# Conditioning loads in the order of need, and a second layer in three groups of units tied to the stream's quarters

## The chip, the cores and the metric

The kernel is one program on one core of a Trainium2 chip. The metric is the device time of one execution in microseconds (us). Before the change it is 3625.27 us, the median of three runs (3622.58 to 3629.86). The engines are named as in the profile: PE is the matrix engine, DVE the vector engine, ACT the scalar engine, POOL the engine that issues the indirect gathers, SP the queue that issues all other transfers.

## The reference

1024 tokens of width 1024 pass two layers. Each layer adds a mixer and then a mixture of experts to h; six vectors a layer (shift, scale and gate for each of the two) come from the conditioning vector c.

```python
c_act = silu(c)
for l in range(2):
    mod = c_act @ ada_w[l] + ada_b[l]                  # 1024 x 6144
    sh1, sc1, g1, sh2, sc2, g2 = split(mod, 6)
    hn = rms_norm(h) * (1 + sc1) + sh1
    if l == 0: mix = hgrn2_mixer(hn)                   # 8 heads, a state carried over the tokens
    else:      mix = stick_breaking_mixer(hn, k_sh, v_sh)   # a block of queries sees all keys before it
    h = h + g1 * mix
    hn = rms_norm(h) * (1 + sc2) + sh2
    h = h + g2 * peer_ffn(hn)
    if l == 0: k_sh, v_sh = split(modulated(rms_norm(h), c_act @ kv_ada_w) @ kv_w, 2)

def peer_ffn(xn):        # per token: 4 heads choose 16 of 16384 experts each
    s1, s2 = top16 of each half of the scores;  best, experts = top16 of the 256 sums
    hid = xn . u[expert]                               # 64 rows of u for each token
    return sum(softmax(best) * gelu(hid) * v[expert])  # 64 rows of v for each token
```

## The kernel before

The tokens are eight blocks of 128. The mixture of experts is a stream that starts in the second tenth of the program and runs to its end: for each layer and block 64 gathers, each of which brings one expert's u and v rows for 128 tokens (8 KB a token, 1 MB a gather) into a tile of the ring g, which has seven buffers. POOL issues the gather (L690), DVE multiplies it with the tokens' rows and sums (L692), ACT makes the weight and a 128 x 32 selection matrix (L694, L696), and PE adds the weighted v rows in PSUM (L699); this last reader sets the buffer free for the gather that is seven later. After 16 gathers DVE takes the sum out (L700). These 16 gathers are a quarter of a block (`peer_quarter`), and the text calls them a **slot**: 64 slots in all, numbered 0 to 63, of which 0 to 31 belong to layer 0.

Beside the stream the other work is done in groups of blocks. Layer 0's mixer (`hgrn_group`, then `mix_route`, which also picks the experts) runs in the groups G0 of two, three and three blocks, and the first of them stands ahead of the stream, because the first gather needs the experts of block 0. Layer 1's attention runs in two groups of four blocks (`attn_group`): queries, eight heads of keys, values and attention, the output (`mix_out`) and the choice of experts (`route_group`). It can start for a group when the stream of layer 0 has finished those blocks, and has to be done before the stream of layer 1 comes to them. Keys and values of the first group are written to memory and read back for the second; the weights are loaded once for each group, 512 KB at a time, into a ring wt of four tiles by SP.

The conditioning is `mod_cols`: each 512 KB piece of the matrix is loaded by SP and multiplied with c_act by one DVE instruction (L215). Twelve vectors of eight pieces (`ada`) and sixteen pieces for the shared keys (`kvada`) make 112 pieces, and all stand ahead of the first gather: 16 of them (`tail_mods`, the last two vectors of layer 1) after the first group's weights of the routing. Pieces after the first sixteen go through halves of one tile of the ring g (`half_tile`).

What decides the order: `at(t)` gives the instructions that follow a due time, and a scheduler orders each engine's instructions by it when the program is built; on the chip every engine then works in that order, and SP issues transfers in that order. T0 and PERIOD place the stream (207 us for a block), W0 the three groups of layer 0, W1 the two of layer 1. `tc.issue_after(x)` puts instructions behind x on their engine. Rings are `BUFS`: T and K are the tiles of a group's activations and of a head's keys, values and scratch; h holds the eight blocks' rows of h.

Of the kernel before, what the change touches and what calls it, by code (L numbers as in the profile page):

```python
# [21 lines left out]
G1 = [[0, 1, 2, 3], [4, 5, 6, 7]]  # L22
GH, GMAX = 3, 4
TAIL = 2
# [12 lines left out]
def tile_model(ctx, tc, x, cin, small, ada, w_in, w_out, kvada, kvw, sbq, sbo, wq, subk, tab0, tab1, out):  # L37
# [9 lines left out]
    BUFS = dict(wt=4, h=8, T=2, K=2, g=7, hn2=1, hq=2, gs=1, st=1)  # L47
# [141 lines left out]
    act_c = unit("hn2")  # L189
# [97 lines left out]
    def mix_out(oT, blocks, w_ap, l, t0, t1):  # L287
        n = len(blocks)
        at(t0)
        for half in range(2):  # L290
            at(t0 + (t1 - t0) * half / 2)
            gsb = mix_row(l, half)
            ws = [wload(w_ap[4 * half + c]) for c in range(4)]
            for i, b in enumerate(blocks):
                at(t0 + (t1 - t0) * (half * n + i) / (2 * n))
                ps = bank()
                for c in range(4):
                    for k in range(8):
                        T.matmul(ps[:, blk(c)], lhsT=oT[:, k, blk(i)], rhs=ws[c][:, k, :], start=(k == 0), stop=(k == 7))  # L299
                V.tensor_tensor(out=ps, in0=gsb, in1=ps, op=ALU.mult)  # L300
                hh = hts[b][:, 512 * half:512 * half + 512]
                V.tensor_tensor(out=hh, in0=hh, in1=ps, op=ALU.add)
# [7 lines left out]
    def hgrn_group(blocks, t0, t1):  # L310
# [27 lines left out]
    def mix_route(oT, blocks, gsb, spare, t0, t1):  # L338
# [7 lines left out]
        early_ws = []  # L346
        if blocks == G0[0]:
            work = [hts[7 - i] for i in range(n)]
            early_ws = hts[2:6]
# [17 lines left out]
        early = 1 if len(held) >= 8 else n  # L367
# [42 lines left out]
    def best_of(l, b, sc):  # L410
        eg = sm("eg", [128, 2, 64], bufs=GMAX)
# [126 lines left out]
    def route_group(l, blocks, t0, t1):  # L538
        at(t0)
# [7 lines left out]
        for j in range(8):  # L547
            at(t0 + 0.4 * (t1 - t0) * j / 8)
# [124 lines left out]
    def peer_quarter(l, b, q):  # L673
# [6 lines left out]
        for c in range(0, 16, NC):  # L680
# [32 lines left out]
    def attn_group(blocks, t0, t1):  # L713
        at(t0)
        d = t1 - t0
# [9 lines left out]
        for j in range(8):  # L725
            at(t0 + d * (0.02 + 0.09 * j / 8))
# [30 lines left out]
        mix_out(qT, blocks, sbo, 1, t0 + 0.7 * d, t0 + 0.8 * d)  # L757
        route_group(1, blocks, t0 + 0.8 * d, t1)
# [28 lines left out]
    def late_mods():  # L787
        mods_out(0)
        mod_cols(modk, kvada, 16, kvb, LATE)
        fold_gain(modk[:, 8:16], kvg)  # L790
        mods_mix(1, LATE)
        mod(1, 2, LATE)
        for m in range(3, 6 - TAIL):
            mod(1, m, LATE)

    def tail_mods():
        with after("tail"), after("wq"):
            for m in range(6 - TAIL, 6):
                mod(1, m, LATE)
# [97 lines left out]
```

## Time and profile before

| what | before |
|---|---|
| median of three runs | 3625.27 us (3622.58 to 3629.86) |
| the profiled execution: its time, its span | 3632.76 us, 3631.1 us |
| busy share PE, DVE, ACT, POOL | 71%, 72%, 31%, 42% |
| mean granted clock of PE | 0.805 |
| DMA: indirect gathers; all else that SP issues | 1073.81 MB, 74.6%; 195.69 MB, 14.3% |
| first gather; end of slot 0, 15, 17, 28, 31, 43, 46, 55 | 335.5; 408.5, 1275.5, 1380.5, 1988.2, 2109, 2783.1, 2932.0, 3299.8 us |

No engine is busy throughout; the busy shares are means over stages, and the slot ends (the start of L700, the first instruction after a slot's last weighted sum) cut the program into them. A DMA share of 1 means that the 16 DMA engines moved data all the time; the granted clock of 1 would be the full 2.4 GHz all the time, and 0.5 the 1.2 GHz.

### The profile page before, as it was taken

The page shows a single profiled execution, that of the slowest core. Times are in us where ns is not written, and L with a number is a line of the kernel's source. Part 1 is how long each engine was busy: PE and PEld are TensorE (multiplying, and loading weights), DVE is VectorE, ACT ScalarE, POOL GpSimd, SP SyncE. Part 2 cuts the span into 40 slices and gives each one's busy share as a digit, 9 for nine tenths or more (in the row PEclk, how much of TensorE's full clock was granted, in tenths as well). Part 3 has the DMA queues.
Part 4 walks back from the last instruction along what each step waited for, and adds up shares of the span by engine and source line. Part 5 has one row for each costly group of instructions (what it writes and reads, how often), then busy time and mean ns, then how long its engine had stood idle before and what let it go on. Part 6 is the DMA issues. An engine that isn't in the chain of part 4 may idle for free.

```text
span 3631.1 us, 52700 instructions
## 1 busy us (share of the span) xinstructions
PE 2585.4 (71%) x18916; PEld 1654.3 (46%) x18916; DVE 2600.6 (72%) x6229; ACT 1127.5 (31%) x2959; POOL 1523.5 (42%) x1691
## 2 busy tenths in 40 slices
PE   5787999878998888988933488788797333343433
PEld 4686666665767745557411135455573111111111
DVE  7949777599776896665799546766757985565555
ACT  2114332233322443333333233333333232222221
POOL 3322656335664333224334433343343444444443
PEclk8898999899999999999955589899998555555555
DMA  9845989897999899888889988887898899999998
GB/s 394 347 143 221 354 344 359 336 352 303 358 361 365 337 344 372 326 337 328 342 349 353 414 352 351 346 328 309 320 381 345 333 373 409 419 415 418 416 416 349
DMA packets 203878, 1272.86 MB, mean 351 GB/s; under 512 B 22626, under 2 KB 22754, under 8 KB 72547
## 3 DMA queue, kind: packets, MB, share of 16 engines
q0 software_dynamic: 147456, 1073.81, 74.6%
q1 hardware_dynamic: 56162, 195.69, 14.3%
q8 instruction: 152, 2.49, 0.3%
q14 instruction: 108, 0.88, 0.1%
HBM read 1261.02 MB, written 8.39 MB: 350 GB/s over the span
## 4 chain that ended last, share of the span: by engine, by line
PE 42%; DVE 28%; issue 13%; POOL 6%; DMA 6%; ACT 5%; POOLq 0%; SPq 0%; DVEq 0%; ACTq 0%; another core or an unknown queue 0%
DVE g L692 8%; PE pj L445 7%; PE va L699 6%; POOL g L690 5%; DMA g<-in_tab_dram,ev 5%; PE pj L730 3%; PE ps L299 3%; PE pj L747 3%; PE pj L552 3%; PE ps L362 2%; ACT hq L668 2%; PE pj L751 2%; PE pj L449 2%; PE po L783 2%; DVE g L215 2%
## 5 line engine op out<-in xcount | busy, mean ns | idle before, releaser
L690 POOL DMA_INDIRECT g<-in_tab_dram,ev x1024 | 1200.7, 1173 | 1720.1 <-PE va L699 1129.0
L692 DVE SCALAR_TENSOR_TENSOR g<-g,hq 128x1024 f32<-128x1024 f32 x1024 | 1260.7, 1239 | 298.7 <-DMA g<-in_tab_dram,ev 287.5
L699 PE MATMUL va<-g,sel 128*32 128x256 f32 x8192 | 751.0, 499 | 772.4 <-ACT sel L696 764.3
L699 PEld LDWEIGHTS va<-g,sel 128*32 128x32 f32 x8192 | 256.7, 132 | 1191.5 <-ACT sel L696 989.3
L694 ACT ACTIVATE w<-hid 128x2 f32<-128x2 f32 x512 | 104.2, 204 | 1293.2 <-DVE g L692 1274.5
L445 PE MATMUL pj<-T,wt 128*128 128x384 f32 (+1 forms) x1152 | 358.7, 462 | 0.0
L668 ACT COPY hq<-hn 32x1024 f32<-32x1024 f32 x256 | 266.8, 1042 | 44.6 <-DVE g L692 40.4
L696 ACT ACTIVATE sel<-dg,w 128x32 f32<-128x32 f32 x1024 | 273.0, 314 | 15.6
L445 PEld LDWEIGHTS pj<-T,wt 128*128 128x128 f32 x1152 | 216.6, 195 | 101.3 <-issue 7.2
L685 DVE TENSOR_TENSOR dg<-delta,gt 128x128 f32<-128x128 f32 x256 | 78.1, 305 | 179.7 <-ACT sel L696 179.2
L494 POOL TENSOR_TENSOR K<-K,F 128x384 f32<-128x384 f32 (+1 forms) x144 | 151.4, 1071 | 52.9 <-DVE T L466 35.4
L215 DVE SCALAR_TENSOR_TENSOR g<-g,hn 128x1024 f32<-128x1024 f32 x104 | 129.2, 1266 | 6.1 <-DMA g<-in_ada_dram 6.1
L449 PE MATMUL pj<-wt,T 128*128 128x128 f32 x1024 | 127.5, 280 | 0.7 <-ACT K L451 0.6
L751 PE MATMUL pj<-wt,T 128*128 128x128 f32 x1024 | 126.3, 277 | 0.0
L751 PEld LDWEIGHTS pj<-wt,T 128*128 128x128 f32 x1024 | 120.0, 192 | 12.7 <-issue 10.6
L449 PEld LDWEIGHTS pj<-wt,T 128*128 128x128 f32 x1024 | 120.5, 194 | 8.8 <-issue 3.7
L299 PE MATMUL ps<-wt,T 128*128 128x128 f32 x1024 | 123.8, 280 | 0.0
L299 PEld LDWEIGHTS ps<-wt,T 128*128 128x128 f32 x1024 | 118.3, 194 | 11.3 <-issue 9.5
L747 PE MATMUL pj<-T,wt 128*128 128x512 f32 x256 | 120.3, 619 | 0.0
L730 PE MATMUL pj<-T,wt 128*128 128x512 f32 x256 | 117.3, 610 | 2.1 <-DVE T L277 2.1
L552 PE MATMUL pj<-T,wt 128*128 128x512 f32 x256 | 116.2, 604 | 0.5 <-DVE T L277 0.5
L783 PE MATMUL po<-K 128*128 128x128 f32 x576 | 104.5, 329 | 15.4 <-ACT K L781 14.9
(239 smaller groups left out, 3896.2 us busy)
## 6 DMA issues: line engine op xcount, KB each, us to landing
wt<-in_w_in_dram SPq DMA_DIRECT2D x96, 512.0 KB
g<-in_ada_dram SPq DMA_DIRECT2D x88, 512.0 KB
g<-in_tab_dram,ev POOLq DMA_INDIRECT x1024
wt<-in_kvw_dram SPq DMA_DIRECT2D x32, 512.0 KB
wt<-in_w_out_dram SPq DMA_DIRECT2D x18, 512.0 KB
wt<-in_wq_dram SPq DMA_DIRECT2D x17, 512.0 KB
g<-in_kvada_dram SPq DMA_DIRECT2D x16, 512.0 KB
wt<-in_sbq_dram SPq DMA_DIRECT2D x16, 512.0 KB
```

Of the source, the lines that this page charges most:

```text
L299: T.matmul(ps[:, blk(c)], lhsT=oT[:, k, blk(i)], rhs=ws[c][:, k, :], start=(k == 0), stop=(k == 7))
L445: T.matmul(pw, lhsT=w[:, k, :], rhs=hT[:, k, 0:W], start=(k == 0), stop=(k == 7))
L449: T.matmul(ps[:, blk(i)], lhsT=hT[:, k, blk(i)], rhs=w[:, k, :], start=(k == 0), stop=(k == 7))
L552: T.matmul(ps[:, 0:128 * n], lhsT=w[:, k, :], rhs=hT[:, k, 0:128 * n], start=(k == 0), stop=(k == 7))
L668: S.copy(t[32 * j:32 * j + 32, :], hn2[32 * q:32 * q + 32, :])
L690: G.indirect_dma_start(out=t, out_offset=None, in_=tab, in_offset=bass.IndirectOffsetOnAxis(ap=ev[:, q, c + k:c + k + 1], axis=0))
L692: V.scalar_tensor_tensor(u, u, 1.0, hq, op0=ALU.mult, op1=ALU.mult, accum_out=hid[:, k:k + 1])
L696: S.activation(sel[:, k, :], dg[:, c % 4 + k, :], AF.Copy, scale=wt[:, k:k + 1])
L699: T.matmul(va[32 * m:32 * m + 32, 0:256], lhsT=sel[:, k, :], rhs=ts[k][:, 1024 + 256 * m:1280 + 256 * m], start=(c + k == 0), stop=(c + k ...
L730: T.matmul(ps[:, 0:W], lhsT=w[:, k, :], rhs=hT[:, k, 0:W], start=(k == 0), stop=(k == 7))
L747: T.matmul(ps[:, 0:W], lhsT=w[:, k, :], rhs=hT[:, k, 0:W], start=(k == 0), stop=(k == 7))
L751: T.matmul(ps[:, blk(i)], lhsT=hT[:, k, blk(i)], rhs=w[:, k, :], start=(k == 0), stop=(k == 7))
```

## The change

**Conditioning.** The 32 pieces of layer 1's vectors 2 to 5 (its mixer's gate and all that its experts need) leave the part ahead of the first gather and are loaded and multiplied inside the hgrn group of blocks 2 to 4, four pieces a head, through the tiles of h that belong to blocks 5 and 6; c_act is kept in block 7's tile so long. The due times of what stays ahead of the first gather are spread (60, 150, 240 in place of 30 and 60), and those of layer 0's groups and of the stream are 40 us earlier. `tail_mods` is gone.

**Layer 1.** The groups are [0,1,2], [3,4,5], [6,7]. `attn_group` becomes a generator that yields after each of twelve units: queries and norms, eight heads, two halves of the output, routing. Behind every slot of the stream from S1 = 17, 29 and 41 on, one unit of that group is put in, and PE's instructions of the unit come behind the last weighted sum of the slot (`after("va")`).

**Tiles.** A group tile T is 3072 columns in place of 4096 for a partition, the ring K has three tiles in place of two, the ring g six in place of seven.

```diff
-G1 = [[0, 1, 2, 3], [4, 5, 6, 7]]
-GH, GMAX = 3, 4
-TAIL = 2
+G1 = [[0, 1, 2], [3, 4, 5], [6, 7]]
+GH, GMAX = 3, 3
-T0, PERIOD = 305.0, 207.0
-W0 = [(5, 230), (250, T0 + 2 * PERIOD - 25), (T0 + 1.8 * PERIOD, T0 + 5 * PERIOD - 60)]
-W1 = [(T0 + 4.7 * PERIOD, T0 + 8.2 * PERIOD), (T0 + 7.9 * PERIOD, T0 + 11.8 * PERIOD)]
+T0, PERIOD = 265.0, 207.0
+W0 = [(5, 240), (210, T0 + 2 * PERIOD - 25), (T0 + 1.8 * PERIOD, T0 + 5 * PERIOD - 60)]
+S1 = [17, 29, 41]
-    BUFS = dict(wt=4, h=8, T=2, K=2, g=7, hn2=1, hq=2, gs=1, st=1)
+    BUFS = dict(wt=4, h=8, T=2, K=3, g=6, hn2=1, hq=2, gs=1, st=1)
...
         for hd in range(8):
             at(t0 + 0.67 * d * hd / 8)
             hgrn_head(n, hd, hT, oT, r8, [])
+            if blocks == G0[1]:
+                m = 2 + hd // 2
+                if hd % 2 == 0:
+                    acc1 = sm("macc", [128, 16])
+                for g in range(4 * (hd % 2), 4 * (hd % 2) + 4):
+                    w = hts[5 + g % 2]
+                    load(w, ada[1, 8 * m + g])
+                    V.scalar_tensor_tensor(w, w, 1.0, act_c, op0=ALU.mult, op1=ALU.mult, accum_out=acc1[:, g:g + 1])
+                if hd % 2:
+                    V.tensor_add(modc[1][:, 8 * m:8 * m + 8], acc1[:, 0:8], adab[:, 48 + 8 * m:56 + 8 * m])
+                    if m == 4:
+                        fold_gain(modc[1][:, 32:40], nfg[:, 8:16])
...
-    def attn_group(blocks, t0, t1):
-        at(t0)
-        d = t1 - t0
+    def attn_group(blocks):
...
+        yield
         for hd in range(8):
-            at(t0 + d * (0.12 + 0.58 * hd / 8))
...
             for i, b in enumerate(blocks):
                 attn_head(b, qT[:, hd, blk(i)], kh, vh, th, st)
-        mix_out(qT, blocks, sbo, 1, t0 + 0.7 * d, t0 + 0.8 * d)
-        route_group(1, blocks, t0 + 0.8 * d, t1)
+            yield
+        for half in range(2):
+            mix_half(qT, blocks, sbo, 1, half)
+            yield
+        route_group(1, blocks)
+        yield
...
-    at(30)
+    at(60)
     mods_ffn(0)
-    at(60)
-    late_mods()
+    at(150)
+    mods_out(0)
+    at(240)
+    mod_cols(modk, kvada, 16, kvb, LATE)
+    fold_gain(modk[:, 8:16], kvg)
+    mods_mix(1, LATE)
...
             peer_quarter(l, b, q)
-        for grp, w in zip(G1, W1):
-            if l == 0 and grp[-1] == b:
-                attn_group(grp, *w)
+            slot = 4 * n + q
+            for first, group in work:
+                if slot >= first:
+                    at(T0 + PERIOD * (slot + 1) / 4)
+                    with after("va"):
+                        next(group, None)
```

Three places show how this moves instructions. The first is SP's queue ahead of the first gather, behind the weights of the first group's routing. Before, it holds the last pieces of conditioning (g is a half tile of the ring g), between the w_in weights (wt) of the second group's heads:

```order
L93 DMA g_398<-in_ada_dram 128x1024 x2
L93 DMA wt_1084<-in_w_in_dram 128x1024
L93 DMA g_403<-in_ada_dram 128x1024 x2
L93 DMA g_408<-in_ada_dram 128x1024 x2
L93 DMA g_415<-in_ada_dram 128x1024 x2
L93 DMA g_420<-in_ada_dram 128x1024 x2
L93 DMA g_425<-in_ada_dram 128x1024 x2
L93 DMA g_430<-in_ada_dram 128x1024 x2
L93 DMA wt_1162<-in_w_in_dram 128x1024
L93 DMA wt_1180<-in_w_in_dram 128x1024
```

With the change, the same place holds the second group's rows (h_142 to h_144 are the tiles of blocks 2 to 4) and the first of the 32 moved pieces, which alternate between the tiles of blocks 5 and 6 (h_145 and h_146):

```order
L93 DMA wt_2327<-in_w_in_dram 128x1024
L93 DMA wt_2345<-in_w_in_dram 128x1024
L93 DMA h_142<-in_x_dram 128x1024
L93 DMA h_143<-in_x_dram 128x1024
L93 DMA h_144<-in_x_dram 128x1024
L93 DMA wt_2359<-in_w_in_dram 128x1024
L93 DMA h_146<-in_ada_dram 128x1024 x4
L93 DMA wt_2387<-in_w_in_dram 128x1024
L93 DMA h_146<-in_ada_dram 128x1024
L93 DMA h_145<-in_ada_dram 128x1024
L93 DMA wt_2490<-in_w_in_dram 128x1024
```

Sixteen pieces are gone from here, and every later piece stands among the weights of its head. The second place is DVE just ahead of the `gt` copy, which is the last thing that the first gather waits for (ev and gt are the experts' numbers and gates of block 0, s and ix the best scores and their places). Before:

```order
L569 MAX_INDEX ix_2151<-s_2150,h_146 128x8
L574 TENSOR_TENSOR cand_2162<-s_2150 128x256
L569 MAX_INDEX ix_2184<-s_2183,h_146 128x8
L613 CAST ev_7255<-pq_7238 128x64
L615 COPY gt_7257<-pq_7238 128x64
```

With the change (h_146 and h_147 in L333 are a moved piece and c_act; lines have moved by six there, so that L621 is the copy that was L615):

```order
L595 SCALAR_TENSOR_TENSOR eg_1829<-e_313_1959 128x16
L571 MAX s_2107<-h_145 128x8 x2
L571 MAX s_2140<-h_145 128x8 x2
L572 MAX_INDEX ix_2108<-s_2107,h_145 128x8 x2
L572 MAX_INDEX ix_2141<-s_2140,h_145 128x8 x2
L333 SCALAR_TENSOR_TENSOR h_146,macc_2480<-h_146,h_147 128x1024
L573 MATCH_REPLACE h_145<-s_2107,h_145 128x128 x2
L573 MATCH_REPLACE h_145<-s_2140,h_145 128x128 x2
L619 CAST ev_7241<-pq_7224 128x64
L621 COPY gt_7243<-pq_7224 128x64
```

The multiplies of moved pieces now stand between the pieces of the top-16 search; three of them stand ahead of this copy. The third place is PE in the middle of a slot that carries a head of layer 1 (va is the stream's weighted sum, T a group's activations, wt weights, K a head's tile, ps and po scores and output of one block's attention). Before, in slot 36:

```order
L783 MATMUL po_16529<-K_16411 128x128 x4
L747 MATMUL pj_16586<-T_15996,wt_16583 128x512 x8
L783 MATMUL po_16529<-K_16411 128x128 x2
L699 MATMUL va_19384<-g_19452,sel_19451 32x256 x4
L699 MATMUL va_19384<-g_19455,sel_19451 32x256 x4
L699 MATMUL va_19384<-g_19474,sel_19473 32x256 x4
L699 MATMUL va_19384<-g_19477,sel_19473 32x256 x4
L783 MATMUL po_16529<-K_16411 128x128
L751 MATMUL pj_16599<-wt_16596,T_15996 128x128 x14
L699 MATMUL va_19384<-g_19494,sel_19493 32x256 x4
L699 MATMUL va_19384<-g_19497,sel_19493 32x256 x4
L751 MATMUL pj_16599<-wt_16596,T_15996 128x128 x12
```

With the change, at the border from slot 23 to slot 24 (L751, L755 and L705 are the lines that were L747, L751 and L699):

```order
L705 MATMUL va_12053<-g_12205,sel_12204 32x256 x4
L705 MATMUL va_12053<-g_12208,sel_12204 32x256 x4
L751 MATMUL pj_12230<-T_10862,wt_12228 128x384 x8
L705 MATMUL va_12374<-g_12380,sel_12379 32x256 x4
L705 MATMUL va_12374<-g_12383,sel_12379 32x256 x4
L755 MATMUL pj_12243<-wt_12241,T_10862 128x128
L705 MATMUL va_12374<-g_12400,sel_12399 32x256 x4
L705 MATMUL va_12374<-g_12403,sel_12399 32x256 x4
L755 MATMUL pj_12243<-wt_12241,T_10862 128x128 x17
L705 MATMUL va_12374<-g_12422,sel_12421 32x256 x4
L705 MATMUL va_12374<-g_12425,sel_12421 32x256 x4
L755 MATMUL pj_12243<-wt_12241,T_10862 128x128 x5
```

Keys for three blocks are eight matmuls of 384 columns in place of 512 for four, and the head's work comes in one run from the border of a slot on, with the stream's weighted sums between its pieces. Before, pieces of the heads stood all over the slot, in the order that the scheduler's due times gave.

## Rows read from the trace of the kernel before

**Rows 1.** The page: busy time, share and instructions of each engine; the queue that SP fills (MB, share).
```profile
PE 2585.4 (71%) x18916; PEld 1654.3 (46%) x18916; DVE 2600.6 (72%) x6229; ACT 1127.5 (31%) x2959; POOL 1523.5 (42%) x1691
...
q1 hardware_dynamic: 56162, 195.69, 14.3%
```

**Rows 2.** Stretches: window, us, busy PE PEld DVE ACT POOL, PEclk, DMA share, GB/s.
```profile
0.00:335.50 335.50, 248.84 (x1539) 221.22 (x1540) 253.01 (x594) 76.65 (x169) 95.13 (x224) 0.89 0.70 268
409.50:1276.50 867.00, 783.60 (x6021) 572.78 (x6020) 679.43 (x1671) 283.95 (x769) 443.89 (x574) 0.95 0.89 345
1276.50:1381.50 105.00, 88.00 (x447) 40.86 (x447) 92.52 (x304) 45.46 (x103) 39.99 (x40) 0.92 0.94 357
1381.50:1989.50 608.00, 450.41 (x3321) 280.84 (x3323) 444.89 (x1234) 206.24 (x539) 217.10 (x196) 0.83 0.89 343
1989.50:2110.50 121.00, 48.80 (x440) 16.96 (x436) 70.91 (x130) 31.96 (x88) 56.83 (x51) 0.53 1.01 412
2110.50:2784.50 674.00, 583.00 (x4027) 372.16 (x4019) 439.81 (x820) 237.39 (x625) 254.30 (x215) 0.93 0.86 336
2784.50:2933.50 149.00, 49.95 (x446) 18.65 (x446) 145.57 (x531) 42.10 (x105) 65.86 (x55) 0.54 0.90 345
2933.50:3301.50 368.00, 145.62 (x1248) 48.77 (x1248) 224.25 (x439) 98.60 (x268) 169.42 (x154) 0.52 1.01 412
3301.50:3632.00 330.50, 125.63 (x1064) 40.30 (x1056) 185.82 (x333) 76.52 (x227) 141.92 (x133) 0.52 0.96 397
```

**Rows 3.** The same stretches, L700 alone (x is the slots that end there), PEclk, DMA share, GB/s.
```profile
409.50:1276.50 867.00, 6.31 (x15) 0.95 0.89 345
1381.50:1989.50 608.00, 4.67 (x11) 0.83 0.89 343
2110.50:2784.50 674.00, 5.13 (x12) 0.93 0.86 336
2784.50:2933.50 149.00, 1.27 (x3) 0.54 0.90 345
2933.50:3301.50 368.00, 3.87 (x9) 0.52 1.01 412
```

**Rows 4.** Timeline around the first gather: start and duration in us, then the instruction.
```profile
335.53 1.23 POOL L690 DMA_INDIRECT g<-in_tab_dram,ev  x1 [29.73 <-DVE gt L615]
...
341.35 1.23 DVE L692 SCALAR_TENSOR_TENSOR g<-g,hq 128x1024 f32<-128x1024 f32 x1 [0.35 <-DMA g<-in_tab_dram,ev]
```

**Rows 5.** The conditioning's multiply, by form: busy us, mean ns, idle before it.
```profile
L215 DVE SCALAR_TENSOR_TENSOR g<-g,hn 128x1024 f32<-128x1024 f32 x104 | 129.2, 1266 | 6.1 <-DMA g<-in_ada_dram 6.1
...
L215 DVE DVE_READ_ACCUMULATOR g<-g,hn 128x1 f32 x104 | 8.4, 81 | 0.0
```

**Rows 6.** Matmuls by form, each trace record standing for one of two per instruction.
```profile
L699 PE MATMUL va<-g,sel 128*32 128x256 f32 x8192 | 751.0, 499 | 772.4 <-ACT sel L696 764.3 <-issue 3.4 <-ACT w L694 3.3
L445 PE MATMUL pj<-T,wt 128*128 128x384 f32 x768 | 265.1, 493 | 0.0
...
L747 PE MATMUL pj<-T,wt 128*128 128x512 f32 x256 | 120.3, 619 | 0.0
L445 PE MATMUL pj<-T,wt 128*128 128x256 f32 x384 | 93.6, 400 | 0.0
```

**Rows 7.** Timeline of one tile of ring g in the stretch that starts at 3301.5 us.
```profile
3303.07 1.05 POOL L690 DMA_INDIRECT g<-in_tab_dram,ev  x1 [0.30 <-issue]
...
3315.70 1.23 DVE L692 SCALAR_TENSOR_TENSOR g<-g,hq 128x1024 f32<-128x1024 f32 x1 [1.21 <-DMA g<-in_tab_dram,ev]
...
3321.38 1.28 POOL L690 DMA_INDIRECT g<-in_tab_dram,ev  x1 [3.62 <-PE va L699]
```

**Rows 8.** Issues of transfers: how many, KB each.
```profile
wt<-in_kvw_dram SPq DMA_DIRECT2D x32, 512.0 KB
...
kD<-K SPq DMA_DIRECT2D x8, 256.0 KB
```

**Rows 9.** Waits over the program: us in all, times, longest.
```profile
POOL g L690 <- PE va L699: 1129.0, 329, 13.9
```

More of the change, by code (lines that the diff above doesn't have):

```diff
@@ L188, in tile_model @@
     V.scalar_tensor_tensor(crow, trow, 1.0, crow, op0=ALU.add, op1=ALU.mult)
-    act_c = unit("hn2")
+    act_c = hts[7]
     for half in range(2):
@@ L285, in mix_row, with mix_half @@
         return g
-    def mix_out(oT, blocks, w_ap, l, t0, t1):
-        n = len(blocks)
-        at(t0)
[L290 to L302, printed above, removed]
+    def mix_half(oT, blocks, w_ap, l, half):
+        gsb = mix_row(l, half)
+        ws = [wload(w_ap[4 * half + c]) for c in range(4)]
+        for i, b in enumerate(blocks):
+            ps = bank()
+            for c in range(4):
+                for k in range(8):
+                    T.matmul(ps[:, blk(c)], lhsT=oT[:, k, blk(i)], rhs=ws[c][:, k, :], start=(k == 0), stop=(k == 7))
+            V.tensor_tensor(out=ps, in0=gsb, in1=ps, op=ALU.mult)
+            hh = hts[b][:, 512 * half:512 * half + 512]
+            V.tensor_tensor(out=hh, in0=hh, in1=ps, op=ALU.add)
     state = unit("st", (128, 8, 128))
@@ L346, in mix_route @@
         early_ws = []
+        if blocks != G0[2]:
+            held += parts(ktile())
         if blocks == G0[0]:
-            work = [hts[7 - i] for i in range(n)]
-            early_ws = hts[2:6]
+            work = [hts[6 - i] for i in range(n)]
+            early_ws = hts[2:5]
         else:
@@ L365, in part_mix @@
             V.tensor_tensor(out=hh, in0=hh, in1=ps, op=ALU.add)
-        early = 1 if len(held) >= 8 else n
+        early = 1 if len(held) > 8 else n
         for half in range(2):
@@ L410, in best_of @@
     def best_of(l, b, sc):
-        eg = sm("eg", [128, 2, 64], bufs=GMAX)
+        eg = sm("eg", [128, 2, 64], bufs=4)
         for j in range(8):
@@ L536, in tile_model, with route_group @@
     norm00, norm7, best0 = [], [], []
-    def route_group(l, blocks, t0, t1):
-        at(t0)
+    def route_group(l, blocks):
         n = len(blocks)
@@ L547, in route_group @@
         for j in range(8):
-            at(t0 + 0.4 * (t1 - t0) * j / 8)
             w = wload(wq[l, j])
@@ L698, in peer_quarter @@
                 for m in range(4):
-                    T.matmul(va[32 * m:32 * m + 32, 0:256], lhsT=sel[:, k, :], rhs=ts[k][:, 1024 + 256 * m:1280 + 256 * m], start=(c + k == 0), stop=(c + k == 15))
+                    last["va"] = T.matmul(va[32 * m:32 * m + 32, 0:256], lhsT=sel[:, k, :], rhs=ts[k][:, 1024 + 256 * m:1280 + 256 * m], start=(c + k == 0), stop=(c + k == 15)).ins
         V.tensor_tensor(out=va[:, 0:256], in0=gates[l], in1=va[:, 0:256], op=ALU.mult)
@@ L725, in attn_group @@
         for j in range(8):
-            at(t0 + d * (0.02 + 0.09 * j / 8))
             w = wload(sbq[j])
@@ L784, in attn_head @@
         S.activation(qT, po[:, 0:128], AF.Copy, scale=0.5)
[L787 to L799, printed above, removed]
-            fold_gain(modc[1][:, 32:40], nfg[:, 8:16])
     at(0)
-    mods_mix(0, ["half"] * 8 + hts[2:] + parts(ktile())[:2])
-    at(30)
+    mods_mix(0, ["half"] * 8 + hts[2:7] + parts(ktile())[:3])
+    at(60)
     mods_ffn(0)
-    at(60)
-    late_mods()
+    at(150)
[4 more added lines that the diff above has]
+    mods_mix(1, LATE)
     for grp, w in zip(G0, W0):
         hgrn_group(grp, *w)
-        if grp is G0[0]:
-            at(240)
-            tail_mods()
     at(200)
@@ L818, in tile_model @@
     order = [(l, b) for l in range(2) for b in range(8)]
+    work = [(first, attn_group(grp)) for first, grp in zip(S1, G1)]
     with tc.issue_after(norm00[0]):
```

2 lines of the change are left out of this document (removed).

## The prediction

> **What bounds the kernel now.** I read the stretches first, because the shares of the page [rows 1] mix stages: PE and DVE look alike there, 71% and 72%, and bound different places. Dividing each stretch [rows 2] by the slots that end in it [rows 3] gives a slot's price by stage. Ahead of the first gather, 335.5 us, nothing streams; DVE is busy 253 of them and the DMA share is 0.70. From 409.5 to 1276.5 us layer 0's groups lie beside the stream: 15 slots of 57.8 us, PE busy 90%, so PE is the bound. While a group of layer 1 runs, slots take 56.2 us (674/12) with PE at 86%, and 55.3 us (608/11) in the first group. Three slots that carry the search for the best experts take 49.7 us with DVE at 98%. With nothing beside the stream a slot takes 40.9 us (368/9), DMA share 1.01: the gathers themselves are the bound, and PE is 40% busy at a granted clock of 0.52. So the program is a sum over slots, and the floor of a slot is 40.9 us. The chain of waits says the same of the stream: the largest wait of POOL is for the weighted sum that frees a buffer [rows 9].
>
> The important thing in these rows is that before, a slot is either full (56 us) or free (41). After the change 26 slots have a head of layer 1 each and are half full. Whether a half-full slot costs as little as its free DMA time allows decides the result.
>
> **Ahead of the first gather.** 16 of 112 pieces leave the part that the group's heads wait for, 16 more leave a place behind its routing. Sixteen pieces are 16 x (1.266 + 0.081) = 21.5 us of DVE [rows 5]; their loads are 16 x 1.39 = 22 us of the DMA engines (14.3% of 3631.1 us for 195.69 MB is 2.65 us a MB [rows 1], so 1.39 us for 512 KB). The stretch is 75% DVE, so not all of DVE's time is on the path: bounds 0 and 22 us. Against it, three moved multiplies stand ahead of the `gt` copy for which the first gather waits [rows 4], 3 x 1.35 = 4 us and some waiting for their loads, 6 in all. I take -22 + 6 = -16: the first gather at 319.5 us. Slot 0 was 73 us (335.5 to 408.5); by the order, 17 us more of layer 0's PE work stand ahead of its end, half of it in PE's idle time: +8, so it ends at 400.5.
>
> **Slots 1 to 17.** Layer 0's PE work is the same, and by the order it now ends with slot 14 in place of 15. A slot takes 11.7 us of stream work on PE (751.0/64 [rows 6]), so the same PE work without that slot is at most 867 - 11.7 = 855 us for slots 1 to 14; by slots it is 14 x 57.8 = 809. I take 840, nearer the PE bound. The 32 moved multiplies, 32 x 1.35 = 43 us, are put at nothing: DVE idles 188 of the 867 us [rows 2]. Without that cover they cost up to 43 us. Slot 15 has the search (55 us), slots 16 and 17 are free (82). Slot 17 ends at 400.5 + 840 + 137 = 1377.5, before 1380.5; the earlier start is nearly given back here, because the stage is bound by PE and slots 15 to 17 were partly filled before (105 us for two [rows 2]).
>
> **Slots 18 to 63.** Before these take 3632 - 1381.5 = 2250.5 us. By the order and the durations of such rows, after has 26 slots with one head (20 to 28, 33 to 40, 44 to 52) and 15 to 26 us of layer work on PE, 19.5 in the mean; 12 with the queries, the output and the routing, mostly 25 to 49 us on PE or 55 to 74 on DVE; and 8 free ones. The same count puts 40 us into each of before's twelve mixed slots. Narrower groups cost PE nothing: 384 columns take 265.1/384 = 0.69 us an instruction, 512 take 120.3/128 = 0.94, 256 take 93.6/192 = 0.49 [rows 6], all 1.8 to 1.9 ns a column.
>
> The bytes: the weights of layer 1 are loaded for three groups in place of two, 16 loads more of kvw beside its 32 [rows 8] and 25 of the others, 21.5 MB; keys and values written and read back grow by 7.3 MB. 28.8 MB x 2.65 = 76 us of DMA engines. In slots with PE as the bound they are hidden (DMA share 0.86 to 0.89); in half-full slots they are not.
>
> A light slot: lower bound, its DMA work alone, 40.9 + 2 loads x 1.39 + 0.39 to 0.79 MB of keys and values x 2.65 = 45. Upper bound, that the layer's PE work costs the stream what it costs now: (56.2 - 40.9) x 19.5/40 = 7.5 more than free, 48.4. I take **46.5**, the middle, since PE with (19.5 + 11.7)/46.5 = 67% is not the bound, but its pieces still come in between. A heavy slot 56.5, as now. A free slot 41.3: 26 x 46.5 + 12 x 56.5 + 330.5 = 2217.5, **-33 us**, of which 76 us of bytes are already paid.
>
> The ring with six buffers: a free slot asks for a gather every 2.56 us, so a buffer of seven comes round in 17.9 us (18.3 in the rows, 3303.07 to 3321.38 [rows 7]), one of six in 15.3. From the multiply to the new issue it takes 5.7 us, so 9.6 remain from issue to multiply; alone a gather takes 5.8 (335.53 to 341.35 [rows 4]). 3.8 us are left in place of 6.4, so free slots stay at 41. The last eight are 330.5 as before.
>
> **The sum.** Span 1377.5 + 2217.5 = 3595; 1.7 us around it make 3597. The profiled execution lies 7.5 us above the median of its runs (3632.76 and 3625.27), so on the median's scale it is **3590 us**. A measurement tells differences from about 0.2%, 7 us.
>
> **A rule against the change.** Rows: the granted clock is 0.52 where PE is 40% busy, 0.83 at 74%, 0.93 at 86% [rows 2]; on that line 67% busy would get 0.75 or so, a mix of 1.2 and 2.4 GHz, and 19.5 us of work become 24, still under the slot's 46.5. The Trainium skill, page "TensorE: Matmul & The Clock Gate", Part 1 on the clock gate, says that the slow clock is the default, that sustained activity lifts it and that idle gaps bring it back. By it, spread heads would run at the slow clock throughout. The trace agrees as far as it goes; no stretch of it shows half-full slots. As a mechanism of this kernel it is part of the third rival.
>
> **The rivals.**
> - *Full filling (0.20).* The head's PE work disappears in the stream's idle PE: light slots 45, heavy 54 (their loads, too, are earlier). -39 - 30 us: 3521. For it: free slots leave PE 60% idle. Against: before, no slot with layer work was under 45.
> - *Work is conserved (0.12).* Each piece costs the stream what it costs now, and the bytes come on top: light 48.4, 3590 + 26 x 1.9 = 3639. For it: the two groups of before differ little per us of work (55.3 and 56.2).
> - *The ring and the border piece (0.13), the slower side.* At each slot's border a piece of 8 x 0.69 = 5.5 us stands ahead of the stream's sums, over the 3.8 us that the ring of six leaves; seven buffers left 6.4. At the clock of the free slots, 0.52 in place of 0.93, the piece is near 10 us and 19.5 us of work are 35, with 16 of stream (145.6/9 [rows 2]) 51. Light slots of 49.8, between: 3590 + 26 x 3.3 = 3676. It decides from a light slot of 47.9 up. Against: PE's order keeps stream sums between the later pieces.
> - *Conditioning waits (0.07).* DVE works in order; a moved multiply whose load is late (two tiles, SP's queue between weights) holds the stream's multiplies behind it: up to +43 us in slots 1 to 14, 3633.
>
> **How the numbers follow.** The forecast as worked out, 3560 to 3618, has 0.36; the same mechanism with light slots of 47.6 to 48.1, within 7 us of before, 0.12. Faster is 0.36 + 0.20 = 0.56; same 0.12; slower 0.12 + 0.13 + 0.07 = 0.32. The likeliest case's own range is 3560 to 3618; the range for 8 in 10 reaches over the rivals on both sides, 3520 to 3685.
>
> **What would show it.** Right: the first gather near 320, slot 17's end near 1378, slots 20 to 28 of 46 to 47 us with a DMA share of 0.95 or more, free slots of 41 with six tiles. Wrong: light slots of 49 or more with a granted clock near 0.55 and more of POOL's wait for the weighted sum; a DVE that waits for loads at L333; or a first gather still at 335, if PE's heads and not the pieces set that stretch (PE is busy 249 of 335.5 us).

## The result and the profile after

The changed kernel takes 3720.43 us (median of four runs, 3716.19 to 3735.8), the kernel before 3627.57 us (3622.58 to 3630.07): a ratio of 1.0271 (95% interval 1.0254 to 1.0288), slower by 93 us between the medians and by 98 us by the ratio. The forecast was 3590 us with a range of 3520 to 3685. The profiled execution took 3716.99 us with a span of 3715.0 us.

The page after, engines and the queue that SP fills:

```profile
PE 2633.0 (71%) x19308; PEld 1770.2 (48%) x19308; DVE 2614.4 (70%) x6229; ACT 1137.9 (31%) x2993; POOL 1530.6 (41%) x1691
...
q1 hardware_dynamic: 66674, 224.53, 16.1%
```

Beside [rows 1] nothing stands out: the same shares, and 28.84 MB more. Stretches of the changed kernel (window, us, busy PE PEld DVE ACT POOL, PEclk, DMA share, GB/s): ahead of the first gather, slots 1 to 14, slots 15 to 17, the three runs of light slots, and the end.

```profile
0.00:319.50 319.50, 249.57 (x1572) 224.15 (x1572) 219.75 (x530) 77.44 (x175) 91.07 (x225) 0.90 0.63 232
404.50:1265.50 861.00, 770.59 (x5843) 569.54 (x5839) 692.31 (x1708) 276.34 (x740) 431.61 (x553) 0.94 0.88 341
1265.50:1405.50 140.00, 46.45 (x386) 14.73 (x387) 101.34 (x286) 37.35 (x95) 59.31 (x49) 0.51 0.93 366
...
1511.00:1955.00 444.00, 290.46 (x2260) 182.15 (x2259) 250.90 (x497) 125.15 (x344) 170.49 (x155) 0.73 0.96 373
2187.50:2593.50 406.00, 286.22 (x2258) 192.85 (x2257) 252.95 (x451) 129.58 (x344) 162.80 (x145) 0.82 0.94 370
2774.50:3221.50 447.00, 276.53 (x2226) 187.65 (x2226) 276.58 (x474) 141.31 (x363) 177.93 (x161) 0.77 0.96 375
...
3366.50:3705.00 338.50, 127.02 (x1072) 40.78 (x1069) 184.68 (x332) 75.32 (x224) 147.25 (x132) 0.52 0.96 388
```

L706, the slots' end, in the light and in six free slots (x is slots), and the first gather:

```profile
1511.00:1955.00 444.00, 3.87 (x9) 0.73 0.96 373
2187.50:2593.50 406.00, 3.42 (x8) 0.82 0.94 370
2774.50:3221.50 447.00, 3.87 (x9) 0.77 0.96 375
3367.50:3627.50 260.00, 2.58 (x6) 0.52 0.97 392
```

```profile
318.29 1.23 POOL L696 DMA_INDIRECT g<-in_tab_dram,ev  x1 [33.62 <-DVE gt L621]
```

The 26 light slots take (444 + 406 + 447)/26 = 49.9 us, the free ones 260/6 = 43.3 where they took 40.8 before (245.0 us for the same six). No engine is the bound in them: PE is busy 65% of the first run, DVE 57%. The DMA share is 0.94 to 0.97 and not the 1.01 of [rows 2]: the DMA engines stand idle for some of the time. Where they do is to be seen at the border of one free slot, from slot 57 to 58, in steps of 2 us (POOL's gathers, then PEclk, DMA share, GB/s), the changed kernel first:

```profile
3447.50:3449.50 2.00, 0.00 (x0) 0.50 1.02 422
3449.50:3451.50 2.00, 0.00 (x0) 0.50 1.01 418
3451.50:3453.50 2.00, 0.12 (x1) 0.50 0.88 365
3453.50:3455.50 2.00, 1.22 (x2) 0.64 0.45 102
3455.50:3457.50 2.00, 1.70 (x2) 1.00 0.87 336
```

The same border in the kernel before:

```profile
3379.50:3381.50 2.00, 0.04 (x1) 0.50 1.01 418
3381.50:3383.50 2.00, 1.23 (x2) 0.50 1.04 422
3383.50:3385.50 2.00, 1.70 (x2) 0.50 0.98 373
```

With six buffers the engines run dry there, with seven they don't. The timeline of the changed kernel says what is late (start, duration, instruction, idle before it):

```profile
3446.55 0.20 ACT L700 ACTIVATE w<-hid 128x2 f32<-128x2 f32 x1 [4.21 <-DVE g L698]
3446.77 4.20 ACT L674 COPY hq<-hn 32x1024 f32<-32x1024 f32 x4
3451.00 0.53 ACT L702 ACTIVATE sel<-dg,w 128x32 f32<-128x32 f32 x2
...
3451.37 1.93 PE L705 MATMUL va<-g,sel 128*32 128x256 f32 x16 [7.27 <-ACT sel L702]
...
3453.38 0.97 POOL L696 DMA_INDIRECT g<-in_tab_dram,ev  x1 [0.34 <-PE va L705]
```

Between the last weight of the slot (L700) and its selection (L702) ACT makes the four copies of the next slot's rows, 4.2 us. PE waits for the selection, and two buffers with it; the next gather goes out 8.2 us after the one at 3445.14 us. Both kernels have these copies there, and before, too, 8.2 us lie between the two gathers at this border (3373.23 and 3381.46 us): what differs is that with a seventh buffer enough gathers are under way to keep the engines busy so long.

Against the sum, by the slot ends of the profiled executions (all in us):

| part | forecast | measured |
|---|---|---|
| first gather | 319.5 | 318.3 |
| slot 0 | 81 | 84.8 |
| slots 1 to 14 | 840 | 862.4 |
| slots 15 to 17 | 137 | 139.8 |
| 26 light slots | 1209 | 1297 |
| 12 heavy slots | 678 | 664 |
| free slots and end | 330.5 | 349 |

### The profile page after: what moved, and what is told of

The parts are those of the page before. It is cut to its first block, busy times and chain, and to the rows that moved or that the text cites. A ratio compares the mean times of both kernels' runs of the same rounds, so it can differ in the third digit from the quotient of the medians.

```text
span 3715.0 us, 53600 instructions
## 1 busy us (share of the span) xinstructions
PE 2633.0 (71%) x19308; PEld 1770.2 (48%) x19308; DVE 2614.4 (70%) x6229; ACT 1137.9 (31%) x2993; POOL 1530.6 (41%) x1691
## 3 DMA queue, kind: packets, MB, share of 16 engines
q1 hardware_dynamic: 66674, 224.53, 16.1%
## 5 line engine op out<-in xcount | busy, mean ns | idle before, releaser
L705 PE MATMUL va<-g,sel 128*32 128x256 f32 x8192 | 727.6, 486 | 782.5 <-ACT sel L702 782.1
L705 PEld LDWEIGHTS va<-g,sel 128*32 128x32 f32 x8192 | 251.2, 129 | 1153.6 <-ACT sel L702 984.6
L700 ACT ACTIVATE w<-hid 128x2 f32<-128x2 f32 x512 | 104.2, 203 | 1275.8 <-DVE g L698 1266.2
L454 PE MATMUL pj<-T,wt 128*128 128x384 f32 (+1 forms) x1152 | 363.0, 464 | 3.4 <-DVE T L277 3.4
L702 ACT ACTIVATE sel<-dg,w 128x32 f32<-128x32 f32 x1024 | 273.1, 314 | 15.1
L751 PE MATMUL pj<-T,wt 128*128 128x384 f32 (+1 forms) x384 | 145.9, 533 | 3.3 <-DVE K L779 2.2
L755 PEld LDWEIGHTS pj<-wt,T 128*128 128x128 f32 x1024 | 125.2, 192 | 22.8 <-issue 14.8
L791 PE MATMUL po<-K 128*128 128x128 f32 x576 | 117.7, 370 | 21.9 <-ACT K L789 21.7
L755 PE MATMUL pj<-wt,T 128*128 128x128 f32 x1024 | 133.0, 279 | 0.0
L788 PE MATMUL ps<-ident,K 128*128 128x128 f32 x288 | 62.5, 363 | 96.1 <-DVE K L782 96.1
L458 PE MATMUL pj<-wt,T 128*128 128x128 f32 x1024 | 129.7, 280 | 0.7 <-ACT K L460 0.6
L791 PEld LDWEIGHTS po<-K 128*128 128x128 f32 x576 | 102.2, 268 | 44.1 <-ACT K L789 39.5
L559 PE MATMUL pj<-T,wt 128*128 128x384 f32 (+1 forms) x384 | 119.8, 462 | 4.0 <-DVE T L277 2.4
```

What stands on the lines that cost most here:

```text
L454: T.matmul(pw, lhsT=w[:, k, :], rhs=hT[:, k, 0:W], start=(k == 0), stop=(k == 7))
L458: T.matmul(ps[:, blk(i)], lhsT=hT[:, k, blk(i)], rhs=w[:, k, :], start=(k == 0), stop=(k == 7))
L702: S.activation(sel[:, k, :], dg[:, c % 4 + k, :], AF.Copy, scale=wt[:, k:k + 1])
L705: last["va"] = T.matmul(va[32 * m:32 * m + 32, 0:256], lhsT=sel[:, k, :], rhs=ts[k][:, 1024 + 256 * m:1280 + 256 * m], start=(c + k == 0), ...
L751: T.matmul(ps[:, 0:W], lhsT=w[:, k, :], rhs=hT[:, k, 0:W], start=(k == 0), stop=(k == 7))
L755: T.matmul(ps[:, blk(i)], lhsT=hT[:, k, blk(i)], rhs=w[:, k, :], start=(k == 0), stop=(k == 7))
```

## The experiments

All ratios are to the kernel before, run beside on the same chip. **Theory A**: six buffers are one too few, with bytes as the rest of a light slot's price. **Theory B**: PE's pieces at the borders cost the stream.

**Six buffers in the kernel before.**

```diff
-    BUFS = dict(wt=4, h=8, T=2, K=2, g=7, hn2=1, hq=2, gs=1, st=1)
+    BUFS = dict(wt=4, h=8, T=2, K=2, g=6, hn2=1, hq=2, gs=1, st=1)
```

> The kernel before with six buffers in ring g in place of seven, nothing else. Theory A (bytes and ring): with six buffers the gathers pause once a slot, so slots with nothing beside them go from 40.9 to about 43.3 us, slots bound by PE hardly change; some 28 slots are free or bound by DVE or DMA, so 50 to 65 us more, 3675 to 3690. Theory B (PE pieces at the slots' borders cost the stream, the ring alone does not): free slots stay at 41 and the time within 10 us of before, 3620 to 3640.

Measured 1.0165 (1.0139 to 1.0191), 60 us, as theory A had it. Six free slots take 261.5 us:

```profile
3353.00:3614.50 261.50, 2.58 (x6) 0.53 0.97 390
```

That is 43.6 each, with the same DMA share of 0.97. There are no units at borders in this kernel, so theory B cannot make this loss. But the loss is not in free slots alone: from the first gather to the end of slot 17 this run takes 1082 us in place of 1045, though slots bound by PE were expected to change hardly at all.

**Seven buffers in the changed kernel**, paid for with the third K tile.

```diff
-    BUFS = dict(wt=4, h=8, T=2, K=3, g=6, hn2=1, hq=2, gs=1, st=1)
+    BUFS = dict(wt=4, h=8, T=2, K=2, g=7, hn2=1, hq=2, gs=1, st=1)
...
-        if blocks != G0[2]:
-            held += parts(ktile())
```

> The changed kernel with two tiles for heads and seven buffers in ring g (the second tile held in the routing of layer 0's groups is left out with it). Theory A: free slots back to 41, light slots from 49.9 to about 48, 3645 to 3665. Theory B: light slots stay within 0.5 us of 49.9 and the time at 3700 or more; the third K tile, if it mattered, would make it slower still.

Measured 0.9999 (0.9984 to 1.0014): the whole loss is gone, more than the 1.005 to 1.011 that theory A's 3645 to 3665 us would be. Its light and free slots:

```profile
1510.00:1929.00 419.00, 3.86 (x9) 0.77 0.99 393
2158.50:2550.00 391.50, 3.43 (x8) 0.82 0.98 383
2725.00:3162.00 437.00, 3.86 (x9) 0.79 0.97 386
3305.50:3554.50 249.00, 2.57 (x6) 0.52 1.01 412
```

Light slots take 48.0 us at nearly the granted clocks of the changed kernel (0.77, 0.82, 0.79 against 0.73, 0.82, 0.77), and the DMA share is up to 0.99: it is the ring and not the clock.

**Two K tiles and six buffers**, to part the ring from the K tile (the edit above, with another last number):

```diff
-    BUFS = dict(wt=4, h=8, T=2, K=3, g=6, hn2=1, hq=2, gs=1, st=1)
+    BUFS = dict(wt=4, h=8, T=2, K=2, g=6, hn2=1, hq=2, gs=1, st=1)
...
```

> The changed kernel with two K tiles and the six buffers of the change: against the run with seven buffers only the ring differs, against the change only K. Theory A (the ring alone): the change's own time, ratio 1.020 to 1.032. If the third K tile had cost the time (by its place in the heads' order), below 1.010.

Measured 1.0311 (1.0291 to 1.0331). The step from seven to six buffers alone is 3.1%; the third K tile is worth some 0.4% (1.0311 against 1.0271), so giving a buffer of g for it was the bad side of a trade.

**Eight buffers**, the same memory as the change:

```diff
-    BUFS = dict(wt=4, h=8, T=2, K=3, g=6, hn2=1, hq=2, gs=1, st=1)
+    BUFS = dict(wt=4, h=8, T=2, K=2, g=8, hn2=1, hq=2, gs=1, st=1)
...
```

> The changed kernel with two tiles for heads and eight buffers (the same bytes of memory as three and six). Theory A, by which seven buffers already keep the DMA share at 0.97 to 0.99 in light slots: 1 us less at most in 26 light slots, some more in slots where a PE piece delays sums, so ratio 0.988 to 0.999 against before. If each buffer were worth as much as the seventh: 85 us less again, 0.977.

Measured 0.9925 (0.9912 to 0.9938), 27 us faster than before and within theory A's range. Light slots take 46.8 us, with a DMA share of 1.01 in the first run:

```profile
1513.00:1915.00 402.00, 3.86 (x9) 0.77 1.01 409
...
3276.00:3517.50 241.50, 2.58 (x6) 0.51 1.01 417
```

**Two units behind each slot**, with six buffers:

```diff
-                    at(T0 + PERIOD * (slot + 1) / 4)
-                    with after("va"):
-                        next(group, None)
+                    for _ in range(2):
+                        at(T0 + PERIOD * (slot + 1) / 4)
+                        with after("va"):
+                            next(group, None)
```

> The changed kernel with two units of layer 1 behind each slot, so that a group takes 6 slots in place of 12. Theory A (light slots are bound by the bytes and by the gathers that they slow, full slots hide both under PE): 18 full slots of 57 to 60 us and 28 free ones of 43.4, about 2260 us in place of 2310 from slot 18 on, 3660 to 3680. Theory B (each piece costs the stream as much wherever it lies): 3710 to 3735.

Measured 1.0332 (1.0315 to 1.035), slower than the change. Both expectations missed. Slots 18 to 23, behind which the first group's units stand two and two, take 56.7 us in the mean, as theory A had it, but the three slots after them stay long as well (55.1 us), with DVE busy 93%. All in all slots 18 to 29 take 632 us here and 603 in the change: packed together, the units cost more than spread out (PE is busy 90% in slots 18 to 23).

**Without the tie to the slot's last sum**, seven buffers:

```diff
...
-                    with after("va"):
-                        next(group, None)
+                    next(group, None)
```

> The kernel with two K tiles and seven buffers, and PE's work of a unit no longer put behind the slot's last weighted sum (due times alone decide). Theory A (DMA is the bound in light slots): within 10 us of the one with seven buffers, ratio 0.997 to 1.003. Theory B (the piece at the border delays the sums): faster by 20 to 50 us, 0.986 to 0.994; if the border keeps PE's pieces from standing ahead of the stream's sums, slower instead.

Measured 1.0176 (1.0162 to 1.019), 64 us slower than with the tie, the last of the cases above. The tie keeps the units in their slots: without it they run early, slots 18 to 38 take 58.6 us in the mean, and nearly all that follow are free. So theory B's gain did not come, but since whole units have moved, the run does not test the piece at the border by itself. The trace of the changed kernel shows this piece in front of the stream's sums, here at the border from slot 23 to 24:

```profile
1704.11 1.93 PE L705 MATMUL va<-g,sel 128*32 128x256 f32 x16 [7.35 <-ACT sel L702]
1705.98 6.08 PE L751 MATMUL pj<-T,wt 128*128 128x384 f32 x16
1711.90 0.61 PE L755 MATMUL pj<-wt,T 128*128 128x128 f32 x4
1712.43 1.93 PE L705 MATMUL va<-g,sel 128*32 128x256 f32 x32
```

From the selection for a slot's first gather to the end of its sum it takes 5.6 us in the mean of the 26 light slots and 1.3 in six free ones, so this piece holds a buffer about as long as the copies do. With seven buffers it takes 5.7, and there the time is that of the kernel before. How much of the light slots' loss with six is due to it was not measured.

**Two groups of four blocks** with the same tie and seven buffers:

```diff
-G1 = [[0, 1, 2], [3, 4, 5], [6, 7]]
-GH, GMAX = 3, 3
+G1 = [[0, 1, 2, 3], [4, 5, 6, 7]]
+GH, GMAX = 3, 4
...
-S1 = [17, 29, 41]
+S1 = [17, 33]
...
```

> Seven buffers, two K tiles, units behind the slots as in the change, but two groups of four blocks (from slots 17 and 33) in place of three groups. 14 loads and the keys and values of the third group less: 28.8 MB less, at 2.65 to 3.9 us a MB 76 to 112 us of DMA work. If bytes set the light slots (theory A), 30 to 70 us faster than seven buffers with three groups, ratio 0.980 to 0.992. If the cost of a unit goes by its PE work and not its bytes, no difference: 0.997 to 1.004.

Measured 1.0067 (1.0055 to 1.008), slower than three groups by 0.7% though it moves 28.8 MB less. Both expectations missed. In all, smaller units are worth more than the third group's bytes cost.

**The conditioning: short multiplies**, six buffers.

```diff
-                    V.scalar_tensor_tensor(w, w, 1.0, act_c, op0=ALU.mult, op1=ALU.mult, accum_out=acc1[:, g:g + 1])
+                    V.scalar_tensor_tensor(w[:, 0:64], w[:, 0:64], 1.0, act_c[:, 0:64], op0=ALU.mult, op1=ALU.mult, accum_out=acc1[:, g:g + 1])
```

> The changed kernel with the 32 moved multiplies on 64 of 1024 columns, their loads as they were (layer 1's gates and experts then use other numbers). If the moved multiplies cost DVE time in slots 1 to 3 (theory C), these three slots go from 221 us to about 185 and the time to 3680 to 3690. If those slots are bound by PE's work that now stands earlier, and the loads (theory D), they stay above 210 and the time at 3705 to 3725.

Measured 1.0226 (1.0207 to 1.0245), as theory D had it. Slot 0 ends 12 us earlier (391 us), but slots 1 to 3 take 223 us and slot 17 ends at 1405 us as in the change: the multiplies by themselves are not what slots 1 to 3 pay.

**The conditioning alone** in the kernel before (seven buffers, old layer 1), with the change's own lines for it:

```diff
...
-    act_c = unit("hn2")
+    act_c = hts[7]
...
+            if blocks == G0[1]:
+                m = 2 + hd // 2
...
-    late_mods()
+    at(150)
+    mods_out(0)
...
```

> The kernel before with the conditioning of the change alone (pieces moved into the second hgrn group, its due times, the tiles that this takes); layer 1, K and the seven buffers as before. Theory D (the stage of slots 1 to 15 is bound by PE, whose work is the same, and only PE's idle time ahead of the first gather can be saved, some 17 us): first gather near 319, ratio 0.993 to 0.998. Theory C (the moved pieces cost as much in slots 1 to 3 as they save ahead of them, or more): ratio 0.999 to 1.006.

Measured 1.003 (1.0019 to 1.0041): slower, as theory C had it. The first gather goes out at 320.0 us in place of 335.5, and slot 17 ends at 1408 us in place of 1380.

**The old conditioning** with eight buffers and the new layer 1, the same lines turned round:

```diff
...
-    act_c = hts[7]
+    act_c = unit("hn2")
...
-            if blocks == G0[1]:
-                m = 2 + hd // 2
...
-    at(150)
-    mods_out(0)
...
+    late_mods()
...
```

> Two K tiles, eight buffers, layer 1 in units as in the change, and the conditioning, its due times and its tiles as before the change. In the pairs so far the moved conditioning costs about 11 us (the kernel before with it alone: 1.0030), so 8 to 20 us faster than with eight buffers alone, ratio 0.987 to 0.990; if the order of layer 0 costs as much here because layer 1 starts no earlier, 0.992 to 0.994.

Measured 0.9854 (0.9838 to 0.9871), 0.7% better than eight buffers alone and more than was expected. Slot 17 ends at 1380 us in place of 1409.

**Old due times, moved conditioning**, eight buffers:

```diff
...
-T0, PERIOD = 265.0, 207.0
-W0 = [(5, 240), (210, T0 + 2 * PERIOD - 25), (T0 + 1.8 * PERIOD, T0 + 5 * PERIOD - 60)]
+T0, PERIOD = 305.0, 207.0
+W0 = [(5, 230), (250, T0 + 2 * PERIOD - 25), (T0 + 1.8 * PERIOD, T0 + 5 * PERIOD - 60)]
```

> Two K tiles, eight buffers, the moved conditioning kept, but T0 and W0 (the due times of the stream and of layer 0's groups) as before the change. If the due times set the longer slots 1 to 15 (theory E, order), 8 to 20 us faster than with eight buffers alone, 0.987 to 0.990; if the loads or multiplies do, no faster, 0.991 to 0.996.

Measured 0.9913 (0.9897 to 0.993), not told apart from eight buffers alone; slot 17 ends at 1409 us again. The due times are not it.

**One load for 32**, eight buffers:

```diff
...
-                    w = hts[5 + g % 2]
-                    load(w, ada[1, 8 * m + g])
-                    V.scalar_tensor_tensor(w, w, 1.0, act_c, op0=ALU.mult, op1=ALU.mult, accum_out=acc1[:, g:g + 1])
+                    w = hts[5]
+                    if hd == g == 0:
+                        load(w, ada[1, 8 * m + g])
+                    V.scalar_tensor_tensor(hts[6], w, 1.0, act_c, op0=ALU.mult, op1=ALU.mult, accum_out=acc1[:, g:g + 1])
```

> Two K tiles, eight buffers, the 32 moved multiplies kept in number and length, but 31 of their 32 loads left out (all multiply one loaded piece, so layer 1's gates and experts use other numbers). If the loads cost time in slots 0 to 4 (theory F: 16 MB at 2.65 us a MB are 43 us of DMA, and SP's queue holds them between the heads' weights), 15 to 40 us faster than with eight buffers alone, 0.981 to 0.988; if PE's work or the multiplies bind there, within 6 us, 0.991 to 0.994.

Measured 0.9913 (0.9895 to 0.9931): no gain in the whole, but slot 17 ends at 1394 us, 15 us earlier; layer 1 gives them back, for a reason that was not looked for.

**One load and short multiplies** together, eight buffers (the edit is against the run above):

```diff
-                    V.scalar_tensor_tensor(hts[6], w, 1.0, act_c, op0=ALU.mult, op1=ALU.mult, accum_out=acc1[:, g:g + 1])
+                    V.scalar_tensor_tensor(hts[6][:, 0:64], w[:, 0:64], 1.0, act_c[:, 0:64], op0=ALU.mult, op1=ALU.mult, accum_out=acc1[:, g:g + 1])
```

> Two K tiles, eight buffers, 31 of 32 moved loads left out and the multiplies on 64 of 1024 columns (layer 1's gates and experts use other numbers). With one load and whole multiplies slot 17 ended at 1394 us, with all loads at 1409, with the old conditioning at 1380. If loads and multiplies together are the cost, slot 17 ends at 1375 to 1385; if it is the order of layer 0's work and its tiles, at 1390 to 1397 as with one load.

Measured 0.9865 (0.9847 to 0.9882); slot 17 ends at 1363 us, below both bounds. From the first gather to the end of slot 17, in us of the profiled executions:

| kernel | first gather | slot 17 ends | between |
|---|---|---|---|
| before | 335.5 | 1380.4 | 1045 |
| eight buffers, old conditioning | 338.7 | 1379.8 | 1041 |
| eight buffers, one load, short multiplies | 325.8 | 1363.0 | 1037 |
| eight buffers, one load | 327.6 | 1394.4 | 1067 |
| eight buffers | 329.4 | 1409.0 | 1080 |
| seven buffers | 319.0 | 1405.6 | 1087 |
| the change | 318.3 | 1405.3 | 1087 |
| before, conditioning alone | 320.0 | 1408 | 1088 |
| before with six buffers | 328.3 | 1410.7 | 1082 |
| two K tiles, six buffers | 315.3 | 1420.9 | 1106 |

(The runs come from several chips, on which the kernel before differs by up to 0.5%, some 5 us of such a stretch.) With seven or eight buffers, moved conditioning costs the slots 39 to 43 us (1080 less 1041 or 1037, and 1088 less 1045), and loads and multiplies have to be gone together for all of it to go. With six buffers the old conditioning, too, takes 1082 us, and with the moved one and two K tiles it is 1106; in the change itself no run parts what conditioning, ring and third K tile do to these slots.

**The copies spread**, in the changed kernel with its six buffers: the four copies are kept in a list and put behind four selections of the slot before (not for the first slot of a block).

```diff
...
+            if c >= 2 and pend:
+                with after("sel"):
+                    S.copy(*pend.pop(0))
```

> The changed kernel (three K tiles, six buffers) with ACT's four copies of the next slot's rows, 1.04 us each, put behind four different selections of a slot in place of in one run between the last weight and the last selection; 48 of 64 slots are changed, the first of each block is as it was. Theory A with its place (the ring of six runs dry at the border because the last selection of a slot waits 4 us for the copies): these slots lose the DMA's gap of 1.5 us or more at the border, free ones 41 to 42 in place of 43.4, ratio 1.005 to 1.016. If six buffers are short all over the slot and the copies are not it: 1.021 to 1.030.

Measured 1.0124 (1.0105 to 1.0142) in place of 1.0271, with nothing else changed. Its light and free slots:

```profile
1496.30:1922.00 425.70, 3.86 (x9) 0.74 0.98 389
2154.50:2559.50 405.00, 3.44 (x8) 0.83 0.94 368
2740.00:3183.00 443.00, 3.86 (x9) 0.77 0.96 381
3330.50:3577.00 246.50, 2.58 (x6) 0.52 1.00 412
```

Free slots are back at 41.1 us with six buffers: their whole loss was the copies. Light slots gained 0.9 us only (49.0), so half of what the seventh buffer gives there (48.0) has other causes. By the DMA packets of the trace the engines stand idle for 2.4 us of a light slot in the changed kernel, 0.8 of them within 4 us of the border and the rest later in the slot; with the copies spread the 0.8 are down to 0.2. Of the whole gain some 15 us come before slot 18, 23 in the light slots and 12 in the last eight and the end.

**The copies spread in the fastest kernel** (two K tiles, eight buffers, old conditioning), by the same lines:

```diff
...
+            if c >= 2 and pend:
+                with after("sel"):
+                    S.copy(*pend.pop(0))
```

> The fastest so far (two K tiles, eight buffers, old conditioning; 0.9854) with the copies spread in the same way. With eight buffers the border is covered in free slots: 0.982 to 0.987; if full and light slots lose time at the border too, 0.975 to 0.982.

Measured 0.9793 (0.9773 to 0.9812): 2.1% faster than before, the fastest of all, and in the second of the two ranges. Light slots take 46.1 us:

```profile
1480.00:1879.50 399.50, 3.86 (x9) 0.76 1.01 409
2103.50:2485.00 381.50, 3.44 (x8) 0.85 0.98 387
2661.50:3077.50 416.00, 3.86 (x9) 0.81 0.98 398
```

## Why the prediction was wrong

**The ring of six was put at nothing, and that was the first wrong step.** The working took a buffer's mean round of 15.3 us, 5.7 from multiply to issue, and found 3.8 us left for landing, "so free slots stay at 41". A mean round is not the worst one: at a slot's border ACT's copies add 4.2 us to the release of two buffers, more than the 3.8 that were left and less than the 6.4 of seven. The rows for it stood in the trace before: in its six free slots a buffer's round takes 17.8 us in the mean, but 23.1 us for a slot's fifteenth gather, which the border holds; the working looked at one round away from it [rows 7]. Free slots went to 43.4, light ones to 49.9 where 46.5 was forecast, 88 us over 26 light slots and 18 over the last eight and the end; the heavy slots came out 14 us below the forecast. The border and its copies are shown for free slots; for light slots the number of buffers is shown as the cause and only a part of it put down to the copies.

**The moved conditioning was put at nothing, the second.** "DVE idles 188 of the 867 us" was taken for cover. The moved multiplies run from 305 to 639 us, from just ahead of the first gather into slot 4. In slots 1 to 3 DVE was idle 47 of 181 us before, so idle time of DVE was there; but PE was busy 177 of these 181 us, and with the change they take 221 us, PE busy 209. The price named for a missing cover, 43 us, is what the pairs with seven and eight buffers show (39 to 43); with six it was not parted from the ring's part. The sum missed slot 17's end by 28 us only: from the first gather on it had 1058 us, 13 more than before for the new order of layer 0's work, and with eight buffers 1037 are enough when the moved loads and multiplies are nearly gone. How loads and multiplies share it stays open: one alone gave back 0 (six buffers) or 15 us (eight), and since the scheduler orders each program anew, such an edit may also move layer 0's PE work. Which wait makes the 43 us is not shown.

**What was right.** The first gather at 318.3 (319.5), slots 15 to 17, and the bytes: 28.84 MB, and 16.1% of 3715.0 less 14.3% of 3631.1 are 79 us of DMA engines (76). The light slot of 46.5 needs a larger ring than the change has: 46.8 with eight buffers, 46.1 with the copies spread as well, but 48.0 with seven, which cover the border of free slots. So what the change does to layer 1 is a gain, as forecast, if a smaller one: with seven buffers it pays for the moved conditioning (0.9999 in all against 1.003 for the conditioning alone), with eight buffers and the old conditioning it is 1.5%, of which the eighth buffer is a part (the kernel before was not run with eight).

**The rivals.** The third had the place (the ring, the border) and the size (49.8 us), and its piece, PE's matmuls at the border, is in the trace. But free slots, which have no such piece, lost 2.5 us each, all but 0.3 of which went with the copies; for light slots its share is open. Its other signs, a granted clock near 0.55 and more of POOL's wait for the weighted sum, did not come (1129.0 us of that wait before [rows 9]). What grew is DVE's wait for gathers to land; in the changed kernel:

```profile
POOL g L696 <- PE va L705: 1136.4, 347, 11.9
DVE g L698 <- DMA g<-in_tab_dram,ev: 476.4, 335, 6.9
```

In the kernel before:

```profile
DVE g L692 <- DMA g<-in_tab_dram,ev: 287.5, 214, 9.1
```

The fourth had the conditioning's 43 us, but not how they come about: it had DVE wait for late loads at L333, and there DVE waits 1.7 us in all. The two were given as cases that exclude each other, and both prices came in part; the range ended at 3685 because no case held two of them. That 3590 + 86 + 43 = 3719 falls on the 3720 measured is luck: by the profiled executions, the misses are 28 us up to slot 17, 88 in the light slots, 18 in the last eight and the end, and -14 in the heavy ones.

The Trainium skill, "TensorE: Matmul & The Clock Gate", Part 1, says that the throttled clock is the default and that activity releases it. The prediction took from it, as a rule against the change, that heads spread over half-full slots would run at the slow clock throughout. The rows show 0.73 to 0.82 in them, near the 0.75 read off the line, so they did not. And in the second run of light slots, at a clock of 0.82 with six buffers and with seven, the time went from 406 to 391.5 us.

## What to carry to other kernels

Size a ring by the longest time from a buffer's use to its release, which is found where a slow side job stands between a consumer's steps, not by the mean round; a buffer too few showed here as a DMA share of 0.97 in place of 1.01 in slots that no engine fills. A small side job in the path that frees buffers can be worth as much as a buffer: four copies spread over a slot gave 1.5% of the 2.7% back. And idle time of the engine that gets moved work is not by itself cover: DVE had 47 idle us in slots 1 to 3, and the stretch up to slot 17 still grew by 39 to 43 us. Rivals that do not exclude each other are added when the range is drawn.

## What the runs showed that was not expected

- Loads beside the gathers seem to cost more than their own time. In the first light run with six buffers, SP's 14.29 MB take 9.0% of 445 us, 2.8 us a MB, but the gathers' own packets also take longer: 86.3% of 445 us for 9 slots is 42.7 us a slot, in place of 99.8% of 368 us for 9 slots, 40.8, when they run alone.
- Putting PE's work of a unit behind the slot's last sum is worth 64 us with seven buffers (1.0176 against 0.9999), since it keeps the units in their slots, though its piece at the border delays the stream's first sums by some 4 us.
- The eighth buffer was worth 0.7% (0.9925 against 0.9999) where seven already kept the DMA share at 0.97 to 0.99.
